# Low parts of the weights all made on VectorE, and selection matrices made by comparing two tensors

## The chip, the cores and the metric

The kernel runs on one core of a Trainium2 chip. The metric is the time that the device takes for one execution, in microseconds, as the median of three runs; smaller is better.

## The reference, cut to what matters

The reference is three transformer blocks in a row on 256 tokens of width 1024, all in fp32. In its second block stands a mixture of experts, and the change is in that part of the kernel. Each token goes to the 2 of 8 experts whose router logits are highest, with gates from a softmax over those two:

```python
logits = xt @ router_w                       # 256 x 8
top_val, top_idx = lax.top_k(logits, 2)
gates = jax.nn.softmax(top_val, axis=-1)
# tokens sorted by expert; each expert on its own rows:
y = (silu(xb @ w1[e]) * (xb @ w3[e])) @ w2[e]    # w1, w3: 1024 x 2816, w2: 2816 x 1024
out = segment_sum(y * gate, token)
```

The other parts (two attention layers, a differential attention with a short convolution, two dense feed-forward layers, a gated mixer and a sparse attention) are matmuls against weights in the same manner, and the change does not touch their code.

## The kernel before

All weights are fp32 and come from device memory. A product in fp32 precision is made of matmuls on a faster number format: a weight tile `raw` of 128 x 1024 is split into a high part `hi`, its value rounded to that format by a copy on ScalarE (L760), and a low part `lo = raw - hi` by a subtraction (L761). The activations are split in the same way. A product then takes three matmuls that add up in one PSUM bank: high by high, low by high, high by low (`mm3`, L786 to L788).

The expert stage goes through the experts in four pairs, (0, 1), (2, 4), (5, 6), (3, 7), and through each expert's hidden width of 2816 in groups of four blocks of 128, with a last group of two. Four groups of the one expert of a pair alternate with four of the other; then come the last two groups of the one and of the other. A turn is a group's products with `w1` and `w3` (`first`) and, after them, the product with `w2` of the group before it (`second`). `Units` gives out the weights for this: 528 units of 128 x 1024 (0.524 MB), in the order of use. Each unit is loaded by SyncE's DMA queue, mostly two with one transfer, and split by `Units.fetch` four units ahead of the matmuls, since there are four buffers for high and four for low parts. So ScalarE's copy for a unit waits for the matmuls of the unit four before it.

Experts 2 and 3 are narrow: they work on 64 rows that hold the high parts of the tokens and 64 that hold the low parts. There, two matmuls make a product (L1738, L1739): with `hi` and with `lo`. Two other steps stand in these turns: TensorE folds the two halves together (L1758), ScalarE makes the silu of that (L1763), VectorE the product (L1764), and both make its high and low parts (L1765, L1766).

Around these, VectorE also makes the hidden values of a wide expert (L1822), low parts of what comes out of PSUM (L857), and adds an expert's result to the residual `h` (L1780). `gather` (L1669) makes the selection matrices `G` for a pair, one matrix of 128 x 128 for each of two token tiles and two experts (L1686): it has a one where a token's place at the expert is the column's number. Matmuls against `G` (L1693) then pick the tokens.

The order of work on TensorE, VectorE and ScalarE in this stage is that in which the code issues it (`in_order` links each instruction to the one before it on its engine). GpSimd and SyncE work through their own queues and wait on semaphores. In the kernel before, `Units.fetch` gives each eighth subtraction (L526) to GpSimd: 66 of 528.

Of the kernel before, what the change touches and what calls it, by code (L numbers as in the profile page):

```python
# [10 lines left out]
F32 = mybir.dt.float32  # L11
# [4 lines left out]
ALU = mybir.AluOpType  # L16
# [4 lines left out]
P = 128  # L21
# [458 lines left out]
class Units:  # L480
# [40 lines left out]
    def fetch(s):  # L521

        if s.n < len(s.todo):
            k = s.k
            hi, lo = k.split(*(s.early.pop(s.n, None) or s.load(s.n, s.where.get(s.n))),
                             sub=k.nc.gpsimd if s.n % 8 == 7 else k.nc.vector)  # L526
            *_, kp, _, c = s.todo[s.n]
            s.ready.append([(c + j, hi[:, j], lo[:, j]) for j in range(kp)])
            s.n += 1
# [53 lines left out]
class K:  # L583
# [160 lines left out]
            o += w  # L744
        return raw, kper, n

    def split(s, raw, kper, n, pad=0, to=None, sub=None):
        nc = s.nc
        m = kper * n
        if to is None:  # L750
            i = s.nhl % len(s.his)
            s.nhl += 1
            hi = s.his[i].tile([P, s.UE], F32R, tag="hi", name=s.nm("hi"))
            lo = s.los[i].tile([P, s.UE], F32R, tag="lo", name=s.nm("lo"))
        else:
            hi, lo = to
        if pad:
            nc.gpsimd.memset(hi[:, m:m + pad].bitcast(F32), 0.0)
            nc.gpsimd.memset(lo[:, m:m + pad].bitcast(F32), 0.0)
        nc.scalar.copy(hi[:, :m], raw[:, :m])  # L760
        (sub or nc.vector).tensor_tensor(out=lo[:, :m], in0=raw[:, :m], in1=hi[:, :m].bitcast(F32), op=ALU.subtract)  # L761
        if pad:
            return hi[:, :m + pad], lo[:, :m + pad]
        v = lambda t: t[:, :m].rearrange("p (k n) -> p k n", k=kper)
        return v(hi), v(lo)
# [903 lines left out]
    def gather(s, pair, narrow):  # L1669


        nc, x = s.nc, s.x
        G, GT = s.t1p([P, 2, 2, P], F32R), s.t1p([P, 2, 256], F32R)
        bx = lambda shape: s.bx.tile(shape, F32R, tag="bx", name=s.nm("bx"))
        half = [c in narrow for c in pair]
        if any(half):
            X = [[bx([P, 8, P]) for _ in range(1 if half[i] else 2)] for i in range(2)]
            ops = X
        else:
            X = [[bx([P, 4, 2, P]) for _ in range(2)] for _ in range(2)]  # L1680
            ops = [[OfTwo(X[q], i) for q in range(2)] for i in range(2)]

        def onehots():
            for t in range(2):
                for i, c in enumerate(pair):
                    nc.vector.tensor_scalar(G[:, t, i], s.c("iota64" if half[i] else "iota128"), x.pos[:, t, c:c + 1], None, op0=ALU.is_equal)  # L1686

        def chunks(j):
            ps = s.mm([P, 2, 256])
            for c in range(2):  # L1690
                cs = slice((j + c) * P, (j + c + 1) * P)
                for n, (t, q) in enumerate(((0, 0), (1, 0), (0, 1), (1, 1))):
                    nc.tensor.matmul(ps[:, c], lhsT=x.N[q][:, t, cs], rhs=G[:, t].rearrange("p i n -> p (i n)"),  # L1693
                                     start=(c == 0 and n == 0), stop=(n == 3), skip_group_check=True)
            if not any(half):
                hi, lo = (X[q][j // 4][:, j % 4:j % 4 + 2].rearrange("p k i n -> p k (i n)") for q in range(2))
                s.split_ps(hi, lo, ps, None)
                return
            for i in range(2):
                if half[i]:  # L1700
                    hi, lo = (X[i][0][:, j:j + 2, 64 * q:64 * q + 64] for q in range(2))
                else:
                    hi, lo = (X[i][q][:, j:j + 2] for q in range(2))
                s.split_ps(hi, lo, ps[:, :, P * i:P * i + hi.shape[2]], None)

        def slots(i):
            ps, r = s.mm([P, 258]), s.ts(1)
            for t in range(2):
                nc.tensor.transpose(ps[:, t * P:(t + 1) * P], G[:, t, i].bitcast(F32), s.ident)
            for t in range(2):  # L1710
                nc.tensor.matmul(ps[:, 256:258], lhsT=G[:, t, i], rhs=x.rR[:, t], start=(t == 0), stop=(t == 1), skip_group_check=True)
            nc.vector.tensor_reduce(r, ps[:, 256:258], axis=AX.X, op=ALU.add)
            nc.scalar.copy(GT[:, i], ps[:, :256])
            return r, GT[:, i]

        return [onehots] + [lambda j=j: chunks(j) for j in range(0, 8, 2)], ops, slots
# [469 lines left out]
```

## Time and profile before

| | |
|---|---|
| median of 3 runs | 1814.4 us (1813.56 to 1816.65) |
| profiled execution | 1815.24 us, its span 1813.4 us |
| TensorE busy | 1744.8 us (96% of the span) |
| VectorE busy | 1373.6 us (76%) |
| ScalarE busy | 1137.6 us (63%) |
| GpSimd busy | 271.6 us (15%) |
| expert stage, first to last subtraction on GpSimd | 651.9 to 1427 us |

PE is TensorE, DVE is VectorE, ACT is ScalarE, POOL is GpSimd, SP is SyncE; PEld is TensorE's weight load, which runs beside its matmuls. Idle time in front of an instruction counts only on the engine that sets the pace, which in most stretches is TensorE here. The ends of matmuls are modelled: a matmul of 512 columns shows 0.39 us and the next may start 0.23 us after it, so a wait that is shorter than the difference does not show as idle time, and the difference of two starts tells more. The profiled execution's own time is what a sum of durations is set against.

### The profile page before, as it was taken

To read this page: it belongs to the slowest core of one execution; us is meant where nothing else is said; L and a number is where in the kernel's file an instruction comes from. 1 tells how busy PE (TensorE), PEld (TensorE's weight loads), DVE (VectorE), ACT (ScalarE), POOL (GpSimd) and SP (SyncE) were. 2 spreads that over 40 slices of the span, in tenths; PEclk is the share of its full clock that TensorE was granted. 3 is DMA by queue.
4 is the path that set the end of the run, shared out by engine and by line. 5 is a ranking of instruction groups with operands and counts; after the bars stand their busy time and mean duration, and the time that the engine had idled before them with its cause. 6 is when DMAs were issued, how large, how long until landed. Compare 5 with 4: busy or idle time off the path is not lost. (4 is left out here: it accounts for less than half of the span.)

```text
span 1813.4 us, 27240 instructions
## 1 busy us (share of the span) xinstructions
PE 1744.8 (96%) x9986; PEld 1487.7 (82%) x9986; DVE 1373.6 (76%) x1978; ACT 1137.6 (63%) x1598; POOL 271.6 (15%) x168
## 2 busy tenths in 40 slices
PE   8999999999999999998999999998999899999998
PEld 7889889999987878887767878886677688889997
DVE  6676779654467689888898998897989788865544
ACT  6365665644456567876787778776878665554443
POOL 1100011010000212221222122221222120001101
PEclk9899999999999999999999999999999899999999
DMA  8535463856547668997899989996998454257540
GB/s 287 176 128 163 145 206 107 277 186 198 176 139 278 265 260 339 379 369 287 326 387 374 348 327 371 371 372 257 359 389 313 140 161 151 71 177 242 183 143 24
DMA packets 127950, 446.63 MB, mean 246 GB/s; under 512 B 11304, under 2 KB 23856, under 8 KB 96960
## 3 DMA queue, kind: packets, MB, share of 16 engines
q1 hardware_dynamic: 127808, 444.81, 68.0%
q8 instruction: 80, 1.31, 0.3%
q14 instruction: 62, 0.51, 0.1%
HBM read 443.71 MB, written 2.63 MB: 246 GB/s over the span
## 5 line engine op out<-in xcount | busy, mean ns | idle before, releaser
L761 DVE TENSOR_TENSOR lo<-raw,hi 128x1024 fp32r<-128x1024 f32 (+1 forms) x762 | 967.3, 1302 | 303.5 <-ACT hi L760 298.9
L760 ACT CAST hi<-raw 128x1024 fp32r<-128x1024 f32 (+1 forms) x828 | 844.5, 1047 | 419.2 <-PE mm L788 132.2
L761 POOL TENSOR_TENSOR lo<-raw,hi 128x1024 fp32r<-128x1024 f32 x66 | 178.5, 2705 | 614.2 <-ACT hi L760 476.4
L786 PE MATMUL ab<-hi,bx 128*128 128x512 f32 (+1 forms) x576 | 218.1, 379 | 0.0
L788 PE MATMUL ab<-lo,bx 128*128 128x512 f32 (+1 forms) x576 | 215.6, 374 | 1.5 <-POOL lo L761 1.3
L786 PE MATMUL mm<-Xh,hi 128*128 128x256 f32 x760 | 214.3, 282 | 1.9 <-DVE Xl L860 1.9
L787 PE MATMUL ab<-hi,bx 128*128 128x512 f32 (+1 forms) x576 | 214.3, 372 | 0.2 <-DVE bx L857 0.2
L788 PE MATMUL mm<-Xl,hi 128*128 128x256 f32 x760 | 213.8, 281 | 0.0
L787 PE MATMUL mm<-Xh,lo 128*128 128x256 f32 x760 | 213.7, 281 | 0.0
L786 PEld LDWEIGHTS mm<-Xh,hi 128*128 128x128 f32 x760 | 143.2, 188 | 3.2 <-ACT hi L760 2.3
L788 PEld LDWEIGHTS mm<-Xl,hi 128*128 128x128 f32 x760 | 145.6, 192 | 0.0
L787 PEld LDWEIGHTS mm<-Xh,lo 128*128 128x128 f32 x760 | 143.1, 188 | 0.9 <-DVE lo L761 0.2
L788 PEld LDWEIGHTS ab<-lo,bx 128*128 128x128 f32 x576 | 108.4, 188 | 24.6 <-POOL lo L761 3.1
L787 PEld LDWEIGHTS ab<-hi,bx 128*128 128x128 f32 x576 | 108.6, 189 | 18.8 <-DVE bx L857 0.5
L786 PEld LDWEIGHTS ab<-hi,bx 128*128 128x128 f32 x576 | 108.6, 188 | 17.0
L788 PE MATMUL acc<-lo,hp 128*128 128x512 f32 x264 | 103.5, 392 | 0.5 <-DVE lo L761 0.2
L786 PE MATMUL acc<-hi,hp 128*128 128x512 f32 x264 | 103.4, 392 | 0.0
L787 PE MATMUL acc<-hi,hp 128*128 128x512 f32 x264 | 103.1, 390 | 0.0
L786 PE MATMUL fil<-Xh,hi 128*128 128x256 f32 (+1 forms) x352 | 101.6, 289 | 1.3 <-ACT b L2075 0.5
L788 PE MATMUL fil<-Xl,hi 128*128 128x256 f32 (+1 forms) x352 | 100.1, 284 | 0.0
L787 PE MATMUL fil<-Xh,lo 128*128 128x256 f32 (+1 forms) x352 | 100.1, 284 | 0.0
L1739 PE MATMUL ab<-lo,bx 128*128 128x512 f32 (+1 forms) x192 | 77.3, 409 | 16.4 <-POOL lo L761 12.2
(521 smaller groups left out, 3169.9 us busy)
## 6 DMA issues: line engine op xcount, KB each, us to landing
raw<-in_moe_dram SPq DMA_DIRECT2D x240, 1024.0 KB, 7.3
raw<-in_ffn_w_dram SPq DMA_DIRECT2D x66, 512.0 KB, 4.5
raw<-in_moe_dram SPq DMA_DIRECT2D x48, 512.0 KB, 7.2
raw<-in_a_w_in_dram SPq DMA_DIRECT2D x24, 512.0 KB, 4.3
raw<-in_w_gate_dram SPq DMA_DIRECT2D x22, 512.0 KB, 4.4
raw<-in_w_up_dram SPq DMA_DIRECT2D x22, 512.0 KB, 4.8
raw<-in_w_down_dram SPq DMA_DIRECT2D x22, 512.0 KB, 3.6
raw<-in_w_in_odd_dram SPq DMA_DIRECT2D x20, 512.0 KB, 4.6
```

What stands on the lines that cost most here:

```text
L760: nc.scalar.copy(hi[:, :m], raw[:, :m])
L761: (sub or nc.vector).tensor_tensor(out=lo[:, :m], in0=raw[:, :m], in1=hi[:, :m].bitcast(F32), op=ALU.subtract)
L786: nc.tensor.matmul(out, lhsT=lh, rhs=rh, start=start, stop=False, skip_group_check=skip)
L787: nc.tensor.matmul(out, lhsT=ll, rhs=rh, start=False, stop=False, skip_group_check=skip)
L788: nc.tensor.matmul(out, lhsT=lh, rhs=rl, start=False, stop=stop, skip_group_check=skip)
L1739: nc.tensor.matmul(out, lhsT=x[0], rhs=lo, start=False, stop=stop)
```

## The change

The subtraction for each eighth unit goes to VectorE as the others do, and the selection matrices are made by a comparison of two tensors, the second of which repeats one column, instead of a comparison of a tensor with a scalar per partition.

```diff
@@ -522,8 +522,7 @@
 
         if s.n < len(s.todo):
             k = s.k
-            hi, lo = k.split(*(s.early.pop(s.n, None) or s.load(s.n, s.where.get(s.n))),
-                             sub=k.nc.gpsimd if s.n % 8 == 7 else k.nc.vector)
+            hi, lo = k.split(*(s.early.pop(s.n, None) or s.load(s.n, s.where.get(s.n))))
             *_, kp, _, c = s.todo[s.n]
             s.ready.append([(c + j, hi[:, j], lo[:, j]) for j in range(kp)])
             s.n += 1
@@ -744,7 +743,7 @@
             o += w
         return raw, kper, n
 
-    def split(s, raw, kper, n, pad=0, to=None, sub=None):
+    def split(s, raw, kper, n, pad=0, to=None):
         nc = s.nc
         m = kper * n
         if to is None:
@@ -758,7 +757,7 @@
             nc.gpsimd.memset(hi[:, m:m + pad].bitcast(F32), 0.0)
             nc.gpsimd.memset(lo[:, m:m + pad].bitcast(F32), 0.0)
         nc.scalar.copy(hi[:, :m], raw[:, :m])
-        (sub or nc.vector).tensor_tensor(out=lo[:, :m], in0=raw[:, :m], in1=hi[:, :m].bitcast(F32), op=ALU.subtract)
+        nc.vector.tensor_tensor(out=lo[:, :m], in0=raw[:, :m], in1=hi[:, :m].bitcast(F32), op=ALU.subtract)
         if pad:
             return hi[:, :m + pad], lo[:, :m + pad]
         v = lambda t: t[:, :m].rearrange("p (k n) -> p k n", k=kper)
@@ -1683,7 +1682,8 @@
         def onehots():
             for t in range(2):
                 for i, c in enumerate(pair):
-                    nc.vector.tensor_scalar(G[:, t, i], s.c("iota64" if half[i] else "iota128"), x.pos[:, t, c:c + 1], None, op0=ALU.is_equal)
+                    nc.vector.tensor_tensor(out=G[:, t, i], in0=s.c("iota64" if half[i] else "iota128"),
+                                            in1=x.pos[:, t, c:c + 1].to_broadcast([P, P]), op=ALU.is_equal)
 
         def chunks(j):
             ps = s.mm([P, 2, 256])
```

The changed kernel has one line less from `fetch` to `onehots`, so that the subtraction is L760 there, the low part from PSUM L856 and the comparison L1685; L1764, L1780 and L1822 keep their numbers.

VectorE, in a pair with a narrow expert, the turn around the `w1` and `w3` products of the narrow expert's group; `lo` are low parts of weight units, `hp` the low part of the hidden values. Before:

```order
L1822 SCALAR_TENSOR_TENSOR sh_8961<-ab_8963,sm_8635,sh_8961 128x512
L761 TENSOR_TENSOR lo_9020<-raw_9017,hi_9019 128x1024
L761 TENSOR_TENSOR lo_9030<-raw_9027,hi_9029 128x1024
L761 TENSOR_TENSOR lo_9040<-raw_9037,hi_9039 128x1024
L761 TENSOR_TENSOR lo_9049<-raw_9037,hi_9048 128x1024
L857 TENSOR_TENSOR hp_9061<-mm_9056,hp_9061 128x512
L761 TENSOR_TENSOR lo_9067<-raw_9064,hi_9066 128x1024
L761 TENSOR_TENSOR lo_9075<-raw_9064,hi_9074 128x1024
L761 TENSOR_TENSOR lo_9085<-raw_9082,hi_9084 128x1024
L761 TENSOR_TENSOR lo_9106<-raw_9103,hi_9105 128x1024
```

Of the change, VectorE at the same place:

```order
L1822 SCALAR_TENSOR_TENSOR sh_8961<-ab_8963,sm_8635,sh_8961 128x512
L760 TENSOR_TENSOR lo_9010<-raw_8996,hi_9009 128x1024
L760 TENSOR_TENSOR lo_9020<-raw_9017,hi_9019 128x1024
L760 TENSOR_TENSOR lo_9030<-raw_9027,hi_9029 128x1024
L760 TENSOR_TENSOR lo_9040<-raw_9037,hi_9039 128x1024
L760 TENSOR_TENSOR lo_9049<-raw_9037,hi_9048 128x1024
L856 TENSOR_TENSOR hp_9061<-mm_9056,hp_9061 128x512
L760 TENSOR_TENSOR lo_9067<-raw_9064,hi_9066 128x1024
L760 TENSOR_TENSOR lo_9075<-raw_9064,hi_9074 128x1024
L760 TENSOR_TENSOR lo_9085<-raw_9082,hi_9084 128x1024
L760 TENSOR_TENSOR lo_9096<-raw_9082,hi_9095 128x1024
L760 TENSOR_TENSOR lo_9106<-raw_9103,hi_9105 128x1024
```

Two subtractions, `lo_9010` and `lo_9096`, have come in, the one behind L1822 and the other as the fourth behind the low part of `hp`; a third comes in further on, just ahead of L1764.

VectorE at the end of the pair (0, 1), where the selection matrices `b` of the pair (2, 4) are made from the number row `cm` and the tokens' places `keep`, before:

```order
L857 TENSOR_TENSOR yp_8301<-acc_6859,yp_8301 128x512
L761 TENSOR_TENSOR lo_8307<-raw_8304,hi_8306 128x1024
L1686 TENSOR_SCALAR b_1544_8271<-cm_5823,keep_6516 128x128 x4
L1780 SCALAR_TENSOR_TENSOR h<-mm_8345,keep_6621,h 128x512
L761 TENSOR_TENSOR lo_8352<-raw_8349,hi_8351 128x1024
```

Of the change, the same place:

```order
L856 TENSOR_TENSOR yp_8301<-acc_6859,yp_8301 128x512
L760 TENSOR_TENSOR lo_8307<-raw_8304,hi_8306 128x1024
L1685 TENSOR_TENSOR b_1544_8271<-cm_5823,keep_6516 128x128 x4
L760 TENSOR_TENSOR lo_8330<-raw_8304,hi_8329 128x1024
L1780 SCALAR_TENSOR_TENSOR h<-mm_8345,keep_6621,h 128x512
L760 TENSOR_TENSOR lo_8352<-raw_8349,hi_8351 128x1024
```

The subtraction `lo_8330` now stands between the four comparisons and L1780. GpSimd's queue is shorter by its subtractions; the orders of TensorE, ScalarE and SyncE are the same in both kernels.

## Rows read from the trace of the kernel before

**Rows 1.** The page, costliest groups: GpSimd's subtractions (busy us, mean ns | idle before).

```profile
L761 POOL TENSOR_TENSOR lo<-raw,hi 128x1024 fp32r<-128x1024 f32 x66 | 178.5, 2705 | 614.2 <-ACT hi L760 476.4
```

**Rows 2.** Busy time by stage: a narrow pair, 33 us in it; last columns clock, DMA share, GB/s.

```profile
825.00:1023.00 198.00, 181.97 (x867) 141.87 (x866) 174.15 (x166) 151.89 (x183) 46.54 (x17) 1.00 0.92 351
896.50:929.80 33.30, 31.27 (x142) 24.10 (x140) 29.76 (x25) 26.70 (x31) 8.23 (x4) 1.00 0.99 382
```

**Rows 3.** TensorE's waits, 620 to 1450 us: total us, times, longest.

```profile
PE ab L1739 <- POOL lo L761: 12.2, 10, 1.9
```

**Rows 4.** Order of time, GpSimd, one period: start us, us, what [idle before <-releaser].

```profile
940.01 2.40 POOL L761 TENSOR_TENSOR lo<-raw,hi 128x1024 fp32r<-128x1024 f32 x1 [10.05 <-PE acc L1739]
950.02 3.12 POOL L761 TENSOR_TENSOR lo<-raw,hi 128x1024 fp32r<-128x1024 f32 x1 [7.61 <-ACT hi L760]
960.56 2.69 POOL L761 TENSOR_TENSOR lo<-raw,hi 128x1024 fp32r<-128x1024 f32 x1 [7.42 <-ACT hi L760]
```

**Rows 5.** Order of time, VectorE, the same period; xN are merged.

```profile
939.87 0.74 DVE L1822 SCALAR_TENSOR_TENSOR sh<-ab,sm,sh 128x512 f32<-128x512 f32 x1
940.91 5.99 DVE L761 TENSOR_TENSOR lo<-raw,hi 128x1024 fp32r<-128x1024 f32 x4 [0.30 <-ACT hi L760]
946.82 0.68 DVE L857 TENSOR_TENSOR hp<-mm,hp 128x512 fp32r<-128x512 f32 x1
...
963.16 0.42 DVE L1764 TENSOR_TENSOR sh<-mm,sh 128x256 f32<-128x256 f32 x1 [2.13 <-ACT sh L1763]
```

**Rows 6.** The same view in narrower stretches: the two subtractions that start beside GpSimd's.

```profile
940.91 2.58 DVE L761 TENSOR_TENSOR lo<-raw,hi 128x1024 fp32r<-128x1024 f32 x1 [0.30 <-ACT hi L760]
...
950.92 3.30 DVE L761 TENSOR_TENSOR lo<-raw,hi 128x1024 fp32r<-128x1024 f32 x1
```

**Rows 7.** Groups by form, VectorE, 400 to 560 us (busy us, mean ns | idle).

```profile
L761 DVE TENSOR_TENSOR lo<-raw,hi 128x1024 fp32r<-128x1024 f32 x54 | 66.1, 1225 | 60.3 <-ACT hi L760 60.2
```

**Rows 8.** Order of time, TensorE's matmuls, 941 to 944 and 948 to 954 us.

```profile
941.40 0.39 PE L1739 MATMUL acc<-lo,hp 128*128 128x512 f32 x1
941.62 0.39 PE L1738 MATMUL acc<-hi,hp 128*128 128x512 f32 x1
942.46 0.50 PE L1739 MATMUL acc<-lo,hp 128*128 128x512 f32 x1 [0.45 <-POOL lo L761]
...
953.19 0.50 PE L1739 MATMUL ab<-lo,bx 128*128 128x512 f32 x1 [1.05 <-POOL lo L761]
```

**Rows 9.** Order of time, all engines, end of the pair (0, 1), 824.7 to 829 us.

```profile
824.80 2.55 POOL L761 TENSOR_TENSOR lo<-raw,hi 128x1024 fp32r<-128x1024 f32 x1 [9.46 <-ACT hi L760]
825.02 3.01 DVE L1686 TENSOR_SCALAR b<-cm,keep 128x128 fp32r<-128x128 f32 x4
...
827.95 0.74 DVE L1780 SCALAR_TENSOR_TENSOR h<-mm,keep,h 128x512 f32<-128x512 f32 x1
...
828.74 0.50 PE L1693 MATMUL mm<-b,Xh 128*128 128x256 f32 x2 [0.79 <-DVE h L1780]
```

**Rows 10.** Order of time, all engines, first turn of the pair (2, 4), 845 to 850 us.

```profile
846.80 2.36 POOL L761 TENSOR_TENSOR lo<-raw,hi 128x1024 fp32r<-128x1024 f32 x1 [19.44 <-PE ab L1739]
...
847.69 2.54 DVE L761 TENSOR_TENSOR lo<-raw,hi 128x1024 fp32r<-128x1024 f32 x1 [2.33 <-ACT hi L760]
...
849.21 0.50 PE L1739 MATMUL ab<-lo,bx 128*128 128x512 f32 x1 [1.94 <-POOL lo L761]
```

**Rows 11.** Order of time, all engines, first full period of that pair, 874 to 877 us.

```profile
872.41 3.43 POOL L761 TENSOR_TENSOR lo<-raw,hi 128x1024 fp32r<-128x1024 f32 x1 [13.15 <-ACT hi L760]
...
874.83 3.23 DVE L761 TENSOR_TENSOR lo<-raw,hi 128x1024 fp32r<-128x1024 f32 x2
```

**Rows 12.** Order of time, TensorE, first wide pair, 652 to 655 and 666 to 669 us.

```profile
654.44 0.50 PE L788 MATMUL ab<-lo,bx 128*128 128x512 f32 x1 [0.50 <-POOL lo L761]
...
668.33 0.50 PE L788 MATMUL ab<-lo,bx 128*128 128x512 f32 x1 [0.84 <-POOL lo L761]
```

**Rows 13.** Order of time, VectorE, 822 to 832 us: a two-tensor instruction of 128 columns.

```profile
831.93 0.28 DVE L857 TENSOR_TENSOR bx<-mm,bx 128x128 fp32r<-128x128 f32 x1
```

## The prediction

> **What bounds the kernel now.** I read the page first, then the busy time by stage, then who waits for whom, and last the order of time in one stretch of the expert stage. The 66 low parts that GpSimd makes take 2705 ns each, 178.5 us in all [rows 1], all of them in the expert stage, where the eight experts run as four pairs. In a wide pair TensorE hardly waits. In a pair that holds a narrow expert (825 to 1023 us, and the same again from 1219.5) it is busy for 181.97 of 198.00 us, and VectorE for 174.15 [rows 2]: 16 us per pair in which TensorE waits, and an engine beside it that is nearly full. TensorE's waits name GpSimd's low part first [rows 3].
>
> The reader is to see two things in the order of time. First, GpSimd takes 2.4 to 3.1 us for what VectorE does in 1.2, and matmuls stand for it [rows 4, 8]. Second, GpSimd does not work beside VectorE. The subtraction on VectorE that starts while GpSimd is at its own takes 2.58 and 3.30 us [rows 6] where the stretch without GpSimd's subtractions has 1225 ns [rows 7]. The first starts at 940.91 and ends at 943.49, and GpSimd had ended at 942.41 [rows 4]: it ended 1.08 us later, about one subtraction's time. So each of GpSimd's subtractions holds up VectorE's next one. The instructions of VectorE that read PSUM (L1822, L857) are not stretched.
>
> **The change part by part.** The 66 subtractions go into VectorE's order, just behind the one before them; the orders of TensorE, ScalarE and SyncE are the same. That the change is not what it says is excluded by that order.
>
> VectorE's account, per period of 33.29 us (the three idle times and three durations of rows 4 added up; 24 units of weights): subtractions start 1.137 us apart (four in 5.99, the first 2.58, so (5.99 - 2.58) / 3) [rows 5, 6]. Three more cost 3.41 us. The stretch that goes is (2.58 - 1.21) + (3.30 - 1.21) = 3.46 us. So VectorE has no more to do than before, and what is left is that each moved part is there earlier. I work that out by place.
>
> (a) A full period, with times as in the trace. VectorE is free from its L1822 at 939.87 + 0.66 = 940.53 [rows 5]. The first moved part runs from 940.53 to 941.75. Matmuls start 0.23 apart, so the one that waited until 942.46 could go at 941.62 + 0.23 = 941.85 [rows 8]: in time. The next four subtractions start at 941.67, 942.81, 943.94 and 945.08, L857 at 946.22 instead of 946.82 [rows 5], the next three at 946.82, 947.96 and 949.09, and the second moved part at 950.23. It ends at 951.45, where GpSimd ended at 953.14. The matmul that waits for it starts at about 951.50 instead of 953.19 [rows 8]: 1.69 us. Up to there the matmuls follow VectorE, one unit for one subtraction. Afterwards TensorE has three matmuls per weight tile again and is the slower one, so the 1.69 us stay. The third moved part is the eighth subtraction behind the second: 950.23 + 8 x 1.137 = 959.33, done at 960.55. L1764 behind it waits for TensorE and ScalarE until 963.16 - 1.69 = 961.47 [rows 5], so it costs nothing; the 2.13 us that VectorE idles there cover it, and without them it would cost 1.14.
> A narrow pair has four such periods. In the first the moved part comes behind L1822 at 874.83 and ends at 876.04, 0.2 us after GpSimd's end (872.41 + 3.43), and the one behind it at 877.18, not 876.92 [rows 11]. There the first 0.60 us are not gained and 0.26 us are lost: 1.69 - 0.60 - 0.26 = 0.83. Per pair 3 x 1.69 + 0.83 = 5.9, for two pairs 11.8 us.
>
> (b) Before each narrow pair the four selection matrices take 3.01 us, since GpSimd is at a low part [rows 9]. Alone they would take about 0.86, and the moved part 1.14 behind them, so L1780 comes at 826.95, not 827.95. The matmul that waits 0.79 us for it [rows 9] (0.95 by start times) goes when TensorE is ready. 0.95 x 2 = 1.9 us.
>
> (c) At 849.21 a matmul has waited 1.94 us for GpSimd, and VectorE idled 2.33 us before 847.69 [rows 10]. VectorE takes the part at 846.8 and has it at 848.0 instead of 849.16: 1.16 x 2 = 2.3 us.
>
> (d) In the first wide pair two matmuls wait 0.50 and 0.84 us [rows 12], 0.66 and 1.01 by start times, and 0.1 for the weight load behind each. VectorE is free there: 1.9 us.
>
> (e) The comparison of two tensors instead of a tensor with a column: no row shows it with both inputs in SBUF. Below: 0.28 us, a two-tensor instruction of 128 columns with one input in PSUM [rows 13]; it is the nearest, and about what the old one takes alone. Above: half of a subtraction of 1024 columns, 0.6 us, 16 x 0.33 = 5 us, of which only those on VectorE's path count. I take 0.
>
> Sum: 11.8 + 1.9 + 2.3 + 1.9 = 17.9 us. The profiled execution took 1815.24 us: 1797.3. The median of the runs is 0.8 lower, so I forecast 1796.5 us.
>
> **The rivals.**
> *VectorE keeps its gaps.* Its account per period changes by 3.41 - 3.46, that is nothing. If its gaps do not shrink (2.13 us before L1764, 0.30 at 940.91 [rows 5]), (a) falls away and 6.1 us are left: 1808.3. For it: VectorE is busy for 88% there. Against: the long gap is a wait for TensorE, which itself waited for GpSimd.
>
> *More goes than I count.* The 16 us of a narrow pair hold small waits that come from VectorE running behind since the stretch. If half of what (a) to (c) leave (16.0 - 8.0) goes too, 8 us more: 1788.5.
>
> *The weights cannot come faster.* A narrow pair reads 132 units of 0.524 MB, 69.2 MB. The 33 us with the highest share, 0.99, move 382 GB/s [rows 2]; 69.2 MB take 181 us at that, and the pair needs 190 after the change. By this row DMA is no bound over a pair, at most for moments: 2 us, 1798.5. The Trainium skill (DMA: Bandwidth & Descriptors, section Bandwidth) has about 358 GB/s for HBM to SBUF as what binds; by it a pair takes 193 us, 3 lost twice, 1802.5. The row with 382 GB/s over 33 us is above that figure.
>
> *Slower: the long subtractions are not GpSimd's doing.* If they come from something else at these places, they stay, and VectorE has 3.41 us more per period where it sets the pace. The gap of 2.13 us at L1764 takes up that much; 1.28 us are left, 8 periods, 10 us, and (b) to (d) bring nothing: 1824.5. It decides from the point where less than 1.28 us of the 3.46 go away. For it: nothing in the trace shows a lock as such. Against: in 400 to 560 us, with no such work on GpSimd, the mean is 1225 ns. One rule speaks for this side: the Trainium skill (Perfetto Trace Analysis, section Optimizing Scalar/DVE Operations) says that with VectorE saturated, giving work to another engine, even GpSimd, may make sense, which this change undoes. It adds that the two share a read port, so that it might not help; rows 4 and 6 show the second half.
>
> **How the numbers follow.** Forecast 0.62, gaps that stay 0.17, more 0.11, weights 0.03, nothing that can be measured (the gains given back at the next buffer) 0.03, slower 0.04. About 0.2%, 3.6 us, is what a measurement of this kernel can tell from no change. The first four give faster, 0.93; I take 0.02 off that for what I do not see and give it to the same: faster 0.91, same 0.05, slower 0.04. The likeliest case alone spans 1791 to 1803; 8 in 10 with the neighbours of both sides and the bound of (e): 1788 to 1808.
>
> **What would show it.** In the profile of the changed kernel every subtraction of 1024 columns on VectorE should take 1.21 to 1.23 us in the expert stage, with no second group above 2 us. TensorE should have no wait for GpSimd there; its waits for VectorE's low part stay, mostly behind L857. The period should be 31.6 us, a narrow pair about 190. The four matrices should take about 0.9 us. The gap before L1764 should shrink to about 1 us. I am wrong if VectorE still has subtractions above 2 us, or if the narrow pairs still take 198 us with TensorE waiting for VectorE for as long as it did for GpSimd, or if waits for a transfer appear before ScalarE's copies.

## The result, and the profile after

The changed kernel takes 1792.54 us (median of four, 1789.64 to 1796.28), the kernel before beside it 1813.98. The ratio is 0.9881, with a 95% interval of 0.9856 to 0.9905: 21.6 us less, between 17.2 and 26.1. Forecast were 1796.5 us, from a sum of 17.9 us. The profiled execution took 1794.63 us, its span 1792.8, which is 20.6 less than before.

The page, busy times and costliest groups:

```profile
PE 1740.4 (97%) x9986; PEld 1487.7 (83%) x9986; DVE 1379.5 (77%) x2044; ACT 1136.2 (63%) x1598; POOL 93.6 (5%) x102
...
L760 DVE TENSOR_TENSOR lo<-raw,hi 128x1024 fp32r<-128x1024 f32 (+1 forms) x828 | 982.0, 1220 | 292.7 <-ACT hi L759 285.1
```

GpSimd is busy for 178.0 us less (271.6 to 93.6), which is its group of [rows 1] (178.5), and VectorE only 5.9 us more (1373.6 to 1379.5), though it makes 66 more subtractions of 1.22 us, 80 us of work. So nearly as much was taken from VectorE as was given to it.

Busy time by stage: the first narrow pair, and one of its full periods, answering [rows 2]:

```profile
823.11:1013.29 190.18, 181.64 (x873) 142.57 (x872) 174.24 (x183) 151.72 (x184) 0.00 (x0) 1.00 0.93 363
891.98:923.52 31.54, 31.00 (x142) 24.05 (x141) 29.53 (x28) 26.56 (x30) 0.00 (x0) 1.00 0.99 394
```

The pair is 8 us shorter and the period went from 33.30 to 31.54 us, with the same 174 us on VectorE. The weights keep up: 394 GB/s.

TensorE's waits, 620 to 1430 us (total us, times, longest), answering [rows 3]:

```profile
PE ab L1739 <- DVE lo L760: 5.8, 10, 0.8
...
PE acc L1739 <- DVE lo L760: 3.3, 4, 1.2
```

No wait for GpSimd's low part is left. Where ten waits of 12.2 us in all stood, ten of 5.8 us stand, and they are for VectorE.

Order of time, VectorE, one period, answering [rows 4 to 6]:

```profile
933.50 0.74 DVE L1822 SCALAR_TENSOR_TENSOR sh<-ab,sm,sh 128x512 f32<-128x512 f32 x1
934.16 5.75 DVE L760 TENSOR_TENSOR lo<-raw,hi 128x1024 fp32r<-128x1024 f32 x5
939.83 0.68 DVE L856 TENSOR_TENSOR hp<-mm,hp 128x512 fp32r<-128x512 f32 x1
940.44 13.70 DVE L760 TENSOR_TENSOR lo<-raw,hi 128x1024 fp32r<-128x1024 f32 x12
955.08 0.42 DVE L1764 TENSOR_TENSOR sh<-mm,sh 128x256 f32<-128x256 f32 x1 [0.94 <-ACT sh L1763]
```

Five subtractions now take 5.75 us, where four took 5.99; the first of the five is the one that GpSimd made at 940.01. The gap ahead of L1764 is 0.94 us, it was 2.13.

The same period on TensorE, answering [rows 8]:

```profile
935.25 0.39 PE L1738 MATMUL acc<-hi,hp 128*128 128x512 f32 x1
935.47 0.46 PE L1739 MATMUL acc<-lo,hp 128*128 128x512 f32 x1
...
941.70 0.50 PE L1739 MATMUL ab<-lo,bx 128*128 128x512 f32 x1 [0.53 <-DVE lo L760]
...
945.11 0.50 PE L1739 MATMUL ab<-lo,bx 128*128 128x512 f32 x1
```

The matmul that waited for the first moved part (942.46 before, 2.59 us after the start of L1822) comes 1.97 us after it; the one for the second (953.19, 13.32 after) comes 11.61 after. What is left is the wait behind L856 at 941.70, which was there before too.

The end of the pair (0, 1), VectorE and TensorE, answering [rows 9]:

```profile
823.11 0.89 DVE L1685 TENSOR_TENSOR b<-cm,keep 128x128 fp32r<-128x128 f32 x4
823.91 1.22 DVE L760 TENSOR_TENSOR lo<-raw,hi 128x1024 fp32r<-128x1024 f32 x1
825.05 0.74 DVE L1780 SCALAR_TENSOR_TENSOR h<-mm,keep,h 128x512 f32<-128x512 f32 x1
...
826.31 0.40 PE L1693 MATMUL mm<-b,Xh 128*128 128x256 f32 x2
```

The four matrices take 0.89 us instead of 3.01, the moved part stands behind them, and L1693 does not wait.

The first turn, and the beginning of the first full period, answering [rows 10, 11]:

```profile
843.85 7.10 DVE L760 TENSOR_TENSOR lo<-raw,hi 128x1024 fp32r<-128x1024 f32 x6 [1.39 <-ACT hi L759]
...
843.87 0.50 PE L1738 MATMUL ab<-hi,bx 128*128 128x512 f32 x1
845.13 0.50 PE L1739 MATMUL ab<-lo,bx 128*128 128x512 f32 x1 [0.76 <-DVE lo L760]
...
871.04 5.75 DVE L760 TENSOR_TENSOR lo<-raw,hi 128x1024 fp32r<-128x1024 f32 x5
...
872.31 0.50 PE L1739 MATMUL acc<-lo,hp 128*128 128x512 f32 x1 [1.23 <-DVE lo L760]
```

The wait of 1.94 us is 0.76 now. At 872.31 TensorE waits for the moved part itself: this is the place where the prediction saw VectorE too late for a full gain.

### The profile page after: what moved, and what is told of

Read it like the earlier page. It is cut to its first block, busy times and chain, and to the rows that moved or that the text cites. A ratio compares the mean times of both kernels' runs of the same rounds, so it can differ in the third digit from the quotient of the medians.

```text
span 1792.8 us, 27215 instructions
## 1 busy us (share of the span) xinstructions
PE 1740.4 (97%) x9986; PEld 1487.7 (83%) x9986; DVE 1379.5 (77%) x2044; ACT 1136.2 (63%) x1598; POOL 93.6 (5%) x102
## 5 line engine op out<-in xcount | busy, mean ns | idle before, releaser
L760 DVE TENSOR_TENSOR lo<-raw,hi 128x1024 fp32r<-128x1024 f32 (+1 forms) x828 | 982.0, 1220 | 292.7 <-ACT hi L759 285.1
L785 PE MATMUL ab<-hi,bx 128*128 128x512 f32 (+1 forms) x576 | 218.1, 379 | 0.0
L786 PE MATMUL ab<-hi,bx 128*128 128x512 f32 (+1 forms) x576 | 214.2, 372 | 0.2 <-DVE bx L856 0.2
L1738 PE MATMUL ab<-hi,bx 128*128 128x512 f32 (+1 forms) x192 | 72.3, 383 | 0.0
```

Of the source, the lines that this page charges most:

```text
L760: nc.vector.tensor_tensor(out=lo[:, :m], in0=raw[:, :m], in1=hi[:, :m].bitcast(F32), op=ALU.subtract)
L785: nc.tensor.matmul(out, lhsT=lh, rhs=rh, start=start, stop=False, skip_group_check=skip)
L786: nc.tensor.matmul(out, lhsT=ll, rhs=rh, start=False, stop=False, skip_group_check=skip)
L1738: nc.tensor.matmul(out, lhsT=x[0], rhs=hi, start=start, stop=False)
```

## The experiments

Seven kernels ran. The table has the lengths of the four pairs in the profiled executions, each from TensorE's first L1693 of a pair to the next, the last one to VectorE's last L1780. So what the selection matrices of a narrow pair cost counts to the wide pair ahead of it. Where an edit adds or takes lines, the line numbers in the views shift by one to three.

| kernel | ratio to before (95%) | (0,1) wide | (2,4) narrow | (5,6) wide | (3,7) narrow |
|---|---|---|---|---|---|
| before | 1 | 190.12 | 197.38 | 197.12 | 210.15 |
| changed | 0.9881 (0.9856 to 0.9905) | 186.43 | 189.72 | 195.42 | 201.58 |
| subtractions alone | 0.9868 (0.9844 to 0.9893) | 187.48 | 189.71 | 195.41 | 201.61 |
| comparison alone | 0.9993 (0.9982 to 1.0005) | 190.18 | 199.17 | 196.17 | 211.38 |
| GpSimd in wide pairs | 0.9923 (0.9902 to 0.9943) | 191.11 | 190.28 | 197.05 | 202.88 |
| GpSimd in narrow pairs | 0.9957 (0.9941 to 0.9974) | 186.44 | 197.01 | 195.42 | 209.47 |
| GpSimd reads | 1.0093 (1.0075 to 1.0111) | 194.92 | 204.65 | 200.57 | 216.58 |
| GpSimd writes | 0.9891 (0.9873 to 0.9908) | 188.47 | 189.82 | 195.44 | 201.61 |
| VectorE twice | 1.0132 (1.0112 to 1.0153) | 193.65 | 206.46 | 201.02 | 216.69 |

**The two halves of the change.** First the changed kernel with the old comparison, then the kernel before with the new one:

```diff
-                    nc.vector.tensor_tensor(out=G[:, t, i], in0=..., in1=x.pos[:, t, c:c + 1].to_broadcast([P, P]), op=ALU.is_equal)
+                    nc.vector.tensor_scalar(G[:, t, i], ..., x.pos[:, t, c:c + 1], None, op0=ALU.is_equal)
```

> All 66 subtractions on VectorE, the matrices compared with a scalar as before. My theory (the whole gain is from the subtractions; the form of the comparison is worth nothing): about 21 us below the kernel before, within 2 us of the changed kernel, the four matrices at 0.27 to 0.29 us each. Rival (the comparison of two tensors brings part of the gain, since it stood stretched at the pair's end): 3 us or more above the changed kernel, with a matrix above 1 us.

> Only the comparison is changed, GpSimd keeps its 66 subtractions. My theory: no change, within 2 us of the kernel before; the first matrix at 825 us is still stretched to about 2.4 us, since both its inputs are in SBUF and GpSimd is at work. Rival (the new form isn't held up by GpSimd): the matrices take 0.28 us each there, and 1.9 us are gained.

The subtractions alone give 1792.26 us, the whole effect. The comparison alone gives 1813.4 against 1813.58: no difference that can be told, with an interval from 3.3 us less to 0.9 more. Undisturbed, one matrix takes 281 ns in the one form and 283 in the other. But the expectation that the new form would be held up beside GpSimd as the old one was is wrong. The second kernel's order of time at the end of the pair (0, 1), GpSimd and VectorE:

```profile
827.80 3.37 POOL L761 TENSOR_TENSOR lo<-raw,hi 128x1024 fp32r<-128x1024 f32 x1 [9.46 <-ACT hi L760]
828.01 0.89 DVE L1686 TENSOR_TENSOR b<-cm,keep 128x128 fp32r<-128x128 f32 x4
828.82 0.74 DVE L1781 SCALAR_TENSOR_TENSOR h<-mm,keep,h 128x512 f32<-128x512 f32 x1
829.48 2.77 DVE L761 TENSOR_TENSOR lo<-raw,hi 128x1024 fp32r<-128x1024 f32 x1
```

Beside the same subtraction on GpSimd the four new comparisons are not held up; GpSimd is, 3.37 us instead of 2.55 [rows 9]. Then L1781 comes (L1780 before), with an input in PSUM, and behind it VectorE's subtraction takes 2.77 us and ends at 832.25, 1.08 us after GpSimd. So the hold-up has moved one place on. TensorE's matmul on the selection matrices no longer waits there and comes 0.95 us earlier, ahead of both narrow pairs, as in the changed kernel. The pairs behind are longer all the same, by 1.79 and 1.23 us (table), and in the first of them nearly all of that is the clock. Busy time by stage, two stretches of the pair (2, 4):

```profile
839.42:842.83 3.41, 3.41 (x11) 2.72 (x11) 2.97 (x5) 1.35 (x3) 0.00 (x0) 0.50 0.34 82
853.08:856.49 3.41, 3.41 (x10) 2.54 (x9) 3.41 (x4) 2.03 (x3) 0.00 (x0) 0.50 0.98 339
```

The granted clock is 0.50 there; it was 1.00 throughout this pair in the kernel before. By the starts of the same matmuls in both traces the two stretches cost TensorE 1.7 us. The profiled execution is also the longest of this kernel's twelve (1819.26 us). So whether the 1.9 us of the rival are won over many executions stays open; the interval has room for them.

**Where the gain sits.** The kernel before, with GpSimd's share kept in the wide pairs alone, then in the narrow pairs alone (132 units are a pair):

```diff
-                             sub=k.nc.gpsimd if s.n % 8 == 7 else k.nc.vector)
+                             sub=k.nc.gpsimd if s.n % 8 == 7 and s.n // 132 % 2 == 0 else k.nc.vector)
```

and `== 1` for the other.

> GpSimd keeps its subtractions in the two wide pairs, and VectorE makes all of them in the two narrow pairs. My theory (the narrow pairs give three quarters and more): 16 us below the kernel before, 4 to 5 above the changed kernel; narrow pairs 190 us, wide pairs as before. Rival (VectorE being spared in the wide pairs helps): as fast as the changed kernel or faster.

> GpSimd keeps its subtractions in the two narrow pairs only. My theory: 4 us below the kernel before (3.1 in the first wide pair, 1.1 in the second); narrow pairs 198 us. Rival: no change, the wide pairs are paced by TensorE alone.

The ratios are worth 14.0 us (10.3 to 17.8) and 7.8 us (4.7 to 10.7): together 21.8, the whole again. Expected were 16 and 4 us; the first lies within the measured interval, the second below it. Busy time by stage, the pairs (0, 1) and (2, 4), of the first:

```profile
640.46:831.57 191.11, 188.88 (x904) 156.72 (x904) 167.06 (x173) 146.54 (x162) 41.86 (x16) 0.99 0.89 334
831.57:1021.84 190.27, 181.37 (x866) 142.04 (x866) 174.24 (x183) 151.09 (x182) 0.00 (x0) 1.00 0.92 362
```

and of the second:

```profile
639.82:826.26 186.44, 186.14 (x903) 155.86 (x904) 168.95 (x189) 146.50 (x162) 0.00 (x0) 1.00 0.90 342
826.26:1023.27 197.01, 182.13 (x867) 142.11 (x866) 173.06 (x167) 151.82 (x182) 44.08 (x16) 1.00 0.92 350
```

A pair has the length that goes with its own busy time on GpSimd (44 or 42 us, or 0), whatever the pair beside it has. So the gain is made pair by pair, and the wide pairs have more of it than expected: in the second kernel's profile they are 3.7 and 1.7 us shorter than before, 5.4 together.

**Is it GpSimd's reading that holds VectorE up?** The rival said that the long subtractions come from something else at these places. The changed kernel, with an extra instruction on GpSimd behind each eighth unit that nobody waits for but the load of the next weights into that buffer: a subtraction of the spent tile from itself, or a fill of it with zeros.

```diff
+            if s.n % 8 == 7:
+                k.nc.gpsimd.tensor_tensor(out=raw[0][:, :D], in0=raw[0][:, :D], in1=raw[0][:, :D], op=ALU.subtract)
```

```diff
+            if s.n % 8 == 7:
+                k.nc.gpsimd.memset(raw[0][:, :D], 0.0)
```

> The changed kernel, and GpSimd besides subtracts each eighth raw tile from itself, after its two readers, into that tile, which nobody reads: 66 instructions on GpSimd that read SBUF and for whose result no matmul waits. Theory A (GpSimd holds up VectorE's subtractions while it is at work): VectorE again has subtractions above 2 us, some 66 to 90 of them, its busy time is 60 us or more higher, and the time is 8 to 25 us above the changed kernel. Theory B (all that counted was the matmuls' wait for GpSimd's late result): VectorE's subtractions may stretch, but the time stays within 3 us of the changed kernel.

> As the run before, but GpSimd fills the spent raw tile with zeros: it writes SBUF and reads nothing. Theory A with a hold-up by reads alone: VectorE's subtractions stay at 1.21 to 1.23 us, and the time within 3 us of the changed kernel. Rival (any work of GpSimd in SBUF holds them up, or the tile's later release does): VectorE's subtractions stretch, or the time rises by as much as in the run before.

The first takes 1832.24 us where before takes 1817.72; by the two ratios that is 38 us over the changed kernel, above the 8 to 25 expected. The second takes 1795.8, as the changed kernel does within the intervals. Groups by form of the first:

```profile
L763 DVE TENSOR_TENSOR lo<-raw,hi 128x1024 fp32r<-128x1024 f32 x814 | 1030.1, 1304 | 271.6 <-ACT hi L762 267.0 <-PE mm L1443 1.5 <-PE mm L1598 1.5
...
L528 POOL TENSOR_TENSOR raw<-raw 128x1024 f32<-128x1024 f32 x66 | 215.2, 3260 | 600.9 <-DVE lo L763 562.0 <-issue 19.5 <-DMA raw<-in_moe_dram 19.4
```

and of the second:

```profile
L763 DVE TENSOR_TENSOR lo<-raw,hi 128x1024 fp32r<-128x1024 f32 x814 | 971.3, 1229 | 289.4 <-ACT hi L762 281.6 <-PE mm L1443 1.5 <-PE mm L1598 1.5
...
L528 POOL MEMSET raw<- 128x1024 f32 x66 | 63.1, 956 | 710.6 <-DVE lo L763 699.7 <-issue 11.0
```

With GpSimd reading, VectorE's 814 subtractions take 1030.1 us; with GpSimd only writing, 971.3. In the expert stage 50 of them take over 1.35 us in the first kernel (41 over 2 us, where 66 to 90 were expected); in the second none takes more than 1.23, though five start while GpSimd is writing. The kernel before has 50 such long ones too. In that kernel and in the one with GpSimd's reads, every one of the 50 starts while a subtraction of GpSimd is at work and ends 1.08 or 1.09 us after it. Nobody needs what GpSimd makes there, and ScalarE's copies wait for a transfer for 0.6 us in the whole stage, as in the changed kernel: it is the hold-up that costs the time. The rival falls. The Trainium skill (SBUF — State Buffer, section Who interferes with whom) says that a VectorE instruction with two inputs in SBUF contends with a GpSimd instruction that reads SBUF, not with one that only writes it, and that one with at most one input in SBUF does not contend, outside the modes in which VectorE uses two ports. A mean of 1304 against 1229 ns here, and the 0.74 us of L1781 beside GpSimd, agree.

**What does VectorE's time cost?** The changed kernel, with 66 extra subtractions on VectorE itself, at the same places.

```diff
+            if s.n % 8 == 7:
+                k.nc.vector.tensor_tensor(out=raw[0][:, :D], in0=raw[0][:, :D], in1=raw[0][:, :D], op=ALU.subtract)
```

> The changed kernel, and VectorE makes 66 further subtractions of the same size (raw tile from itself, into that tile, which nobody reads), right behind each eighth one: what it costs when VectorE's account does not cancel. Theory (VectorE sets the pace in the narrow turns for part of each period; 2 of 3 lie in it, and 2.3 us more per period come out): 16 to 26 us above the changed kernel, nearly all in the narrow pairs, wide pairs within 3 us. Rival (VectorE has room): within 5 us.

It takes 1839.46 us, by the ratios 45 over the changed kernel; 16 to 26 were expected, nearly all in the narrow pairs, so that was wrong. Order of time, VectorE, one period:

```profile
944.17 1.21 DVE L763 TENSOR_TENSOR lo<-raw,hi 128x1024 fp32r<-128x1024 f32 x1
945.42 1.23 DVE L528 TENSOR_TENSOR raw<-raw 128x1024 f32<-128x1024 f32 x1
...
966.70 1.23 DVE L528 TENSOR_TENSOR raw<-raw 128x1024 f32<-128x1024 f32 x1
967.84 0.42 DVE L1767 TENSOR_TENSOR sh<-mm,sh 128x256 f32<-128x256 f32 x1
```

There is no gap ahead of the silu product (L1767 here, L1764 before), and the starts of L1767 are 34.15 us apart, where they were 31.56: of three extra subtractions, 3.41 us, 2.6 come out in the period. The gap of 0.94 us is all the cover there is. Beyond it VectorE sets the pace of a narrow pair, and each subtraction more costs nearly its full time. GpSimd's three reads per period give the same period, 34.13 us: a hold-up by GpSimd and a subtraction of its own cost VectorE alike.

What the expectation had wrong is the rest. The wide pairs, which were to stay within 3 us, are 7.2 and 5.6 us longer (table); about 1 us of the 7.2 is a stretch at a clock of 0.50 at its start. Busy time by stage, the pair (5, 6):

```profile
1034.31:1235.34 201.03, 196.36 (x942) 162.14 (x941) 196.52 (x196) 151.66 (x166) 0.00 (x0) 1.00 0.92 347
```

VectorE is busy for 196.52 of 201.03 us there, so it has next to no room in a wide pair either. In the narrow pairs the parts outside the full periods grow too.

## Why the prediction was right, point by point

The place, the mechanism and the side were right. 17.9 us lie within the measured interval, at its lower end; the profiles say where the rest is. One reading was too wide: that each of GpSimd's subtractions holds up VectorE's next one. Of 66, 50 do, and two more hold up a matrix; the third one of the period in the working [rows 4] runs mostly in VectorE's gap ahead of L1764, and its sum rightly counts two.

| step | predicted | changed against before |
|---|---|---|
| (a) from the first to the last L1764 of four periods, both pairs | 5.9 + 5.9 | 6.06 + 5.99 |
| (b) from L1779 to L1693, ahead of both narrow pairs | 0.95 + 0.95 | 0.94 + 0.96 |
| (c) from L1693 to the first L1764, both | 1.16 + 1.16 | 1.36 + 2.14 |
| (d) first wide pair, to its last L1779 | 1.9 | 2.75 |
| the same in the second wide pair | 0 | 0.74 |
| from the last L1764 to the end of a narrow pair | 0 | 0.25 + 0.44 |
| ahead of the stage, and behind it | 0 | -1.26 + 0.26 |
| sum | 17.9 | 20.6 |

**(a)** held to the tenth. The first period was to gain 0.83 us and the three others 1.69 each: in the first three, L1764 went from 37.48, 33.31 and 33.26 us apart to 36.66, 31.54 and 31.56, gains of 0.82, 1.77 and 1.70. In the period of the working, L1764 was to start 21.60 us behind L1822; it starts 21.58 behind. The account behind it, 3.41 us added against 3.46 taken away, is borne out from the other side by the two kernels that add the one or the other and reach the same period. That what is left is GpSimd's late results is read from the matmuls that waited for them; no kernel here takes away the lateness alone.

**(b)** held to 0.01 us, with the order as forecast: L1780 1.94 us behind the first matrix (1.93 worked out).

**(c)** held for the matmul that it is about. Before, that one starts 2.44 us (first pair) and 2.43 us (second) behind the one ahead of it, and in the changed kernel 1.26 us in both: 1.18 and 1.17 us, where 1.16 were forecast. The first pair, before:

```profile
846.77 0.49 PE L1738 MATMUL ab<-hi,bx 128*128 128x512 f32 x1
849.21 0.50 PE L1739 MATMUL ab<-lo,bx 128*128 128x512 f32 x1 [1.94 <-POOL lo L761]
```

As a stretch, (c) was too small in the second narrow pair, 2.14 instead of 1.16. The reason is the clock. Busy time by stage, before, from just behind TensorE's wait at 1241.5 to 1243.7 us:

```profile
1244.20:1247.60 3.40, 3.40 (x10) 2.62 (x9) 3.40 (x4) 2.48 (x3) 0.00 (x0) 0.51 0.84 306
```

The granted clock there is 0.51, the lower of TensorE's two levels (1.2 GHz), after a turn with several waits of which the last is 1.94 us long; eight matmuls start 0.43 us apart instead of 0.23. In the changed kernel the same turn shows 1.00 throughout, and so it does with the subtractions alone and with GpSimd's writes. The first narrow pair of before has the same wait of 1.94 us and no such stretch behind it, and (c) is 0.78 us less there. So the wait alone does not bring the clock down. Such stretches also stand where GpSimd has no share: one in the second narrow pair with GpSimd in the wide pairs (at 1228.18 us), two in the first narrow pair with VectorE's extra subtractions (836.55 and 850.20). Whether the change itself keeps the clock up in that turn is therefore not shown; the 0.78 us may be luck of the execution that was profiled. The prediction had not looked at the clock of that turn.

**(d)** and the second wide pair are the terms that were too small: 1.9 and 0 us forecast, 2.75 and 0.74 found. The waits of [rows 12] are gone; so are shorter ones that were not counted because the page shows little or no idle time for them. One of them, TensorE before, in the pair (5, 6):

```profile
1068.80 0.39 PE L787 MATMUL acc<-hi,hp 128*128 128x512 f32 x1
1069.42 0.50 PE L788 MATMUL acc<-lo,hp 128*128 128x512 f32 x1 [0.24 <-DVE lo L761]
1069.76 0.39 PE L786 MATMUL acc<-hi,hp 128*128 128x512 f32 x1
```

It starts 0.62 us after the one ahead, and the next 0.34, where 0.23 is the pace: 0.50 us for a wait that shows as 0.24. The table of lengths keeps this within bounds: the first wide pair varies by 2 us among kernels with the same order (186.43 to 188.47), the second by 0.03. About 1 us of the 2 is again the clock: the two longer ones have 3.4 us at 0.50 at the start of that pair, the kernels with 186.43 and 186.44 none. As means over the kernels of the table's first six rows and that with GpSimd's writes, a pair in which GpSimd makes low parts is longer than one in which it makes none by 3.3 and 1.4 us (wide) and 8.0 and 8.4 (narrow), 21.0; the prediction's shares are 2.85 and 0.95, 7.05 and 7.05. These means hold stretches at the lower clock: by the kernels without one in that pair, (0, 1) has 3.7 and (2, 4) 7.3; in (3, 7) every kernel with GpSimd's share has one. So no step failed: the narrow pairs' terms held to a few tenths apart from the clock, and the wide pairs' were small because only waits that show in the profile were counted.

**(e)** is not contradicted: the subtractions alone bring the whole gain, and the ratio of the comparison alone is worth between -3.3 and +0.9 us. Both forms take 0.28 us undisturbed; that they behave differently beside GpSimd was not foreseen.

**The rivals.** VectorE's gaps did shrink, 2.13 to 0.94 us, about 1 as announced, because TensorE comes earlier. That VectorE is the engine that this hangs on is shown by the kernel in which the gap is gone. The weights were no bound: 394 GB/s over a period, above the row of before and above the figure weighed there. "More than I count" is partly true: the two narrow pairs, with (b), give 18.1 us where 16.0 were counted, 2.1 more instead of 8, and part of that is the clock. The small waits of TensorE behind L856 did stay. The slower rival is refuted by the kernel with GpSimd's reads that nobody needs. From 640 to 1413 us no subtraction on VectorE is above 1.35 us now; the five in the whole span that are, up to 4.1 us, all lie at or before 631 us beside other work on GpSimd.

What stays open is the -1.26 us ahead of the stage: its first L1693 lies between 634.20 and 640.61 us among kernels that share that code, so it is the spread of that earlier part and not the change.

## What to carry to other kernels

Before work is given to GpSimd to relieve VectorE, look at the VectorE instruction beside each GpSimd one. Here, where VectorE subtracted one SBUF tile from another and GpSimd read SBUF too, one of them stood still, so that the relief came to nothing while the result came later. Work out the balance for one period, instruction by instruction, and follow the two engines to the matmul that waits; that gave the gain of each period of the changed kernel to within 0.1 us. For the size of a small wait take the difference of two starts. Before a difference of 1 or 2 us between two profiles is put down to an edit, compare the granted clock of the two stretches.

## What the runs showed of the hardware

- Which engine gets through first differs from place to place. In the kernel with GpSimd's reads, GpSimd's extra subtraction takes 1.90 us where it is shortest, but 6.16 in this place, GpSimd and VectorE:

```profile
917.25 6.16 POOL L528 TENSOR_TENSOR raw<-raw 128x1024 f32<-128x1024 f32 x1 [10.66 <-DVE lo L763]
...
921.57 0.68 DVE L859 TENSOR_TENSOR hp<-mm,hp 128x512 fp32r<-128x512 f32 x1
922.17 2.32 DVE L763 TENSOR_TENSOR lo<-raw,hi 128x1024 fp32r<-128x1024 f32 x1
```

  It stands through the rest of VectorE's four subtractions from 917.03 and goes on when VectorE turns to L859, which reads PSUM; the subtraction behind that then ends 1.08 us after GpSimd. Elsewhere in that kernel GpSimd gets in between two subtractions (one at 928.03 takes 2.75 us). On average it takes 3.26 us. What decides it is not settled by these runs.
- Comparing with a scalar per partition, the first matrix ahead of each narrow pair took 2.42 us beside GpSimd's subtraction, which took 2.55 and 2.56. Comparing two tensors, it took 0.28 us, and GpSimd's subtraction 3.37 and 3.32. In both kernels GpSimd had started about 0.2 us before the first matrix.
- Filling 128 x 1024 with zeros takes GpSimd 956 ns, and none of VectorE's subtractions in that stage takes more than 1.23 us.
